# A decoder block on one core: the first modulation vectors divided between TensorE and VectorE, and GpSimd's share of that phase given to VectorE and ScalarE

## The chip, the cores and the metric

The kernel runs on one core of a Trainium2 chip. The metric is the device time of one execution in microseconds (us), lower is better. The times shown are device times of whole executions; the profile is of one further execution.

## The reference

One decoder block on x of 512 tokens by 2048 channels, all in float32. A conditioning vector c gives six modulation vectors, of which the first two (shift and scale) are needed before anything else can be projected. Cut to what the change touches:

```python
c_act = silu(c)
mod = c_act @ w_ada + b_ada                    # 2048 x 12288
sh1, sc1, gt1, sh2, sc2, gt2 = split(mod, 6)
h = rms_norm(x, g_mix) * (1 + sc1) + sh1
z = h @ w_in                                   # 2048 x 11344
# z is cut into q, k, v of two attention branches, an indexer's q and k, gates
...
```

Two attention branches, their gated merge, an output projection and a gated feed-forward with a depthwise convolution follow; the change leaves all of them alone.

## The kernel before

Activations stand transposed: a tile is 128 channels by 512 tokens, and there are 16 such channel tiles (the contraction tiles k of w_in). Every float32 product is made of three matmuls (`mm3`, lines 330 to 332): each factor is split into a rounded part h and a remainder l, and h·h, h·l and l·h are summed. ScalarE makes the rounded part of a weight tile (`convert`, L227), and another engine subtracts (L228): GpSimd where the unit is marked `early`, VectorE elsewhere.

The first phase, `first_*` and `hidden`, is a pipeline over the 16 channel tiles in nine groups (`GR`: one tile, seven times two, one). A group g needs the two modulation vectors of its own channels only, and then does a first part of the products for four column blocks of w_in (`FIRST`, in the order given by `ORD`): the indexer's first 512 columns, its 80 columns of k and w, its second 512 columns, and 512 columns of q and k of the first pair of heads. That is 13 output tiles of 128 (one of 80) columns by 512 tokens. Five of the 13 stay in PSUM over all groups ("stay"); eight are taken out of PSUM after each group and added to a copy in SBUF (`evac`, with `late` holding the one that is still to be taken out). PSUM has eight banks.

The modulation vectors of a group are c_act times 16 blocks of w_ada: one block per k, each 128 partitions by 2 vectors by 256 columns (for a group of two). `first_ada` is a generator that handles one block (or two half-size ones) per step. Before the change a step multiplies the block by its c value per partition on VectorE and adds it to one of two accumulators (L670, L672, scalar_tensor_tensor); at the end the two are added (L676). Only in group 0 the first `PK` = 10 blocks go to TensorE instead (L696). `hidden` then sums the accumulator over partitions on TensorE with a column of ones as the moving operand (L696, matmuls of one column; a float32 matmul has two records in the profile), adds the bias (L698), makes the scale (L700), and ScalarE applies scale and shift to the normalised tile `xr` twice (L705 for the rounded part, L711 in place); `hidden_rest_` subtracts (L721). `scaled` makes `xr` by multiplying with the norm (L652): the first two on VectorE, the others on GpSimd.

What sets the order: instructions stand on each engine's queue in the order in which the Python program issues them; nothing reorders them. `paced` runs steps of `first_ada` after each column block, so that the steps of group g+1 are spread over the column blocks of group g; `LEAD` says how many steps it is ahead. `hidden` of the next group is issued after two of the four column blocks of a group (`OF` = 2), `hidden_rest_` after three. Weight loads (`load`, L192) and w_ada loads (`first_load`, L288) are both on SyncE's queue; w_ada is loaded up to `AHEAD` = 10 blocks ahead, w_in three units ahead into three buffers. `evac` takes a tile from PSUM in two ways: for four of the eight keys VectorE adds straight from PSUM (L737), for the other four ScalarE copies (L740) and GpSimd adds (L741).

Of the kernel before, what the change touches and what calls it, by code (L numbers as in the profile page):

```python
# [14 lines left out]
OP = mybir.AluOpType  # L15
# [21 lines left out]
TAB = 640  # L37
NSLOT = 65
AHEAD = 20
LEAD = 8  # L40
AHEAD = 10
OF = 2
SP0 = 22
# [43 lines left out]
PK = 10  # L87
# [17 lines left out]
def block_kernel(ctx, tc, x, c, w_ada, b_ada, g_mix, w_in, w_o_sb, w_o_dsa, w_out, rel_bias,  # L105
                 g_ffn, w_gate, w_up, conv_w, conv_b, w_down, g_final, buckets, out, dbg=None):
    nc = tc.nc
    x, w_ada, w_in, w_o_sb, w_o_dsa, w_out = x[0], w_ada[0], w_in[0], w_o_sb[0], w_o_dsa[0], w_out[0]
# [15 lines left out]
    def T(dt=F32):  # L124
        return slots.tile([128, 512], dt, tag="slot", name="slot")

    def ps():
        return psum.tile([128, 512], F32, tag="ps", name="ps")
# [11 lines left out]
    def U(w, k0, nk, c0, nn, fn, early=False):  # L140
        steps.append(((w, k0, nk, c0, nn, early), fn))
        units.append(steps[-1][0])
# [9 lines left out]
    def F(fn):  # L152
        steps.append((None, fn))
# [5 lines left out]
    def advance(q, n=1):  # L159
        while q and n > 0:  # L160
            try:
                next(q[0])
                n -= 1
            except StopIteration:
                q.pop(0)
# [111 lines left out]
    GROUPS = [(sum(GR[:i]), sum(GR[:i + 1])) for i in range(len(GR))]  # L277
# [5 lines left out]
    def first_load(n):  # L283
        while len(first_raw) < min(n, len(first_cols)):
            k0, k1, k, nk = first_cols[len(first_raw)]
            raw = T().rearrange("p (k v n) -> p k v n", k=nk, v=2)
            for i in range(nk):
                nc.sync.dma_start(raw[:, i], wav2[:, k + i, SH1:SC1 + 1, 128 * k0:128 * k1])  # L288
            first_raw.append(raw)
# [6 lines left out]
    ones = const.tile([128, 128], F32, name="ones")  # L296
# [32 lines left out]
    def mm3(o, sh, sl, mh, ml, start, stop, skip=False):  # L329
        nc.tensor.matmul(o, lhsT=sh, rhs=mh, start=start, stop=False, skip_group_check=skip)  # L330
        nc.tensor.matmul(o, lhsT=sh, rhs=ml, start=False, stop=False, skip_group_check=skip)  # L331
        nc.tensor.matmul(o, lhsT=sl, rhs=mh, start=False, stop=stop, skip_group_check=skip)  # L332
# [221 lines left out]
    fin = []  # L554
# [64 lines left out]


    hT, xT, xr, xT_d = [], [], [], []
    rb1, direct = [], []
    modv2 = modv[:, 0:2 * KT].rearrange("p (v a) -> p v a", v=2)

    def first_norm():
# [22 lines left out]
    def scaled(d1):  # L648

        for d in range(len(xr), min(d1, KT)):  # L650
            xr.append(T())
            (nc.vector if d < 2 else nc.gpsimd).tensor_mul(xr[d], xT[d], rb1[0])  # L652

    fin, seen = [], [0]

    def first_ada():

        for n, (k0, k1, k, nk) in enumerate(first_cols):
            first_load(n + min(AHEAD, 22 - len(hT)))
            if k == 0:  # L660
                acc = []
            for i in range(nk):
                a = first_raw[n][:, i]
                c = c_act[:, k + i:k + i + 1]
                if k0 == 0 and k + i < PK:

                    direct.append((a, c))
                elif len(acc) < 2:
                    acc.append(T()[:, 0:256 * (k1 - k0)].rearrange("p (v n) -> p v n", v=2))
                    nc.vector.tensor_scalar(acc[-1], a, c, None, op0=OP.mult)  # L670
                else:
                    nc.vector.scalar_tensor_tensor(acc[i + k & 1], a, c, acc[i + k & 1], op0=OP.mult, op1=OP.add)  # L672
            first_raw[n] = None
            if k + nk == KT:
                if k0 > 1:
                    nc.vector.tensor_add(acc[0], acc[0], acc[1])  # L676
                    acc.pop()
                fin.append(acc)
            seen[0] += 1
            yield  # L680

    def hidden(k0, k1):

        while not fin:
            advance(back)
        acc = fin.pop(0)
        while late:
            evac(*late.pop())
        n = k1 - k0
        p = ps()  # L690
        terms = direct + [(a, ones[:, 0:1]) for a in acc]
        direct.clear()
        for m, (a, c) in enumerate(terms):
            for v in range(2):
                for i in range(n):
                    nc.tensor.matmul(p[:, v * n + i:v * n + i + 1], lhsT=a[:, v, 128 * i:128 * (i + 1)], rhs=c,  # L696
                                     start=m + v + i == 0, stop=m == len(terms) - 1, skip_group_check=True)
        nc.vector.tensor_add(modv2[:, :, k0:k1], p[:, 0:2 * n].rearrange("p (v a) -> p v a", v=2),  # L698
                             vecs[:, 0:2 * KT].rearrange("p (v a) -> p v a", v=2)[:, :, k0:k1])
        nc.vector.scalar_tensor_tensor(smix[:, k0:k1], modv[:, SC1 * KT + k0:SC1 * KT + k1], 1.0,  # L700
                                       vecs[:, 96 + k0:96 + k1], op0=OP.add, op1=OP.mult)
        for d in range(k0, k1):
            s, b = smix[:, d:d + 1], modv[:, SH1 * KT + d:SH1 * KT + d + 1]
            h, l, u = T(F32R), T(F32R), xr[d]
            nc.scalar.activation(h, u, AF.Identity, scale=s, bias=b)  # L705
            if d == 0:
                y = T()
                nc.vector.tensor_scalar(y, u, s, b, op0=OP.mult, op1=OP.add)
                u = y
            else:  # L710
                nc.scalar.activation(u, u, AF.Identity, scale=s, bias=b)  # L711
            rest.append((l, u, h))
            xr[d] = None
            hT.append((h, l))
# [3 lines left out]
    def hidden_rest_():  # L718
        while rest:
# [5 lines left out]
    FIRST = [(C_QIX, 512, [(2, 256, 128, False), (3, 384, 128, False), (0, 0, 128, True), (1, 128, 128, True)]),  # L725
             (C_QIX + 512, 512, [(6, 256, 128, False), (7, 384, 128, False), (4, 0, 128, True), (5, 128, 128, True)]),
             (C_KIX, 80, [("kw", 0, 80, True)]),
             ((C_QSB, C_KSB), 512, [("q0", 0, 128, False), ("q1", 128, 128, False), ("k0", 256, 128, False), ("k1", 384, 128, False)])]
    part, late = {}, []
    FIRST = [FIRST[i] for i in ORD]  # L730

    def evac(key, p, gi, w):
        if gi == 0:
            part[key] = T()
            nc.scalar.copy(part[key][0:w, :], p)
        elif key in (2, 6, "q0", "k0"):
            nc.vector.tensor_add(part[key], part[key], p)  # L737
        else:
            t = T()
            nc.scalar.copy(t, p)  # L740
            nc.gpsimd.tensor_add(part[key], part[key], t)  # L741

    def first_go(h, l, gi, tiles):
        k0, k1 = GROUPS[gi]
        for key, off, w, stay in tiles:
            if not stay:
                p = ps()[0:w, :]
            elif gi == 0:
                p = part[key] = ps()[0:w, :]
            else:  # L750
                p = part[key]
            for k in range(k0, k1):
                mm3(p, h[:, k - k0, off:off + w], l[:, k - k0, off:off + w], *hT[k],
                    k == 0 if stay else k == k0, k == KT - 1 if stay else k == k1 - 1)
            if late:
                evac(*late.pop())
            if not stay:
                late.append((key, p, gi, w))

    def spill(d1):  # L760

        for d in range(len(xT_d), min(d1, len(xr))):
            xT_d.append(dram.tile([128, 512], F32, name=f"xT{d}"))
            nc.sync.dma_start(xT_d[d], xT[d])
            xT[d] = None

    def paced(gi, i):

        goal = base[gi + 1] + LEAD
        if gi + 1 < len(GROUPS):  # L770
            goal += (i + 1) * (base[gi + 2] - base[gi + 1]) // (len(FIRST) - OF + 1)
        while seen[0] < min(goal, base[-1]):
            advance(back)

    base = [sum(16 // (2 // (b - a)) for a, b in GROUPS[:g]) for g in range(len(GROUPS) + 1)]
# [15 lines left out]
    for gi, (k0, k1) in enumerate(GROUPS):  # L791
        for i, (c0, nn, tiles) in enumerate(FIRST):
            if i == len(FIRST) - OF and gi + 1 < len(GROUPS):
                F(lambda g=gi + 1: hidden(*GROUPS[g]))
            if i == len(FIRST) - OF2:
                F(hidden_rest_)
            U(w_in, k0, k1 - k0, c0, nn, lambda h, l, gi=gi, tiles=tiles: first_go(h, l, gi, tiles), True)
            F(lambda gi=gi, i=i: paced(gi, i))
            F(lambda d=k1 + 4: scaled(d))
            F(lambda d=4 * gi + i - SP0: spill(d))  # L800

# [666 lines left out]
    acc = {}  # L1468
# [226 lines left out]
    held, last = [], []  # L1695
# [61 lines left out]
```

## Time and profile before

| | |
|---|---|
| time, median of 3 runs | 3073.22 us (3072.06 to 3073.41) |
| profiled execution, its own time | 3069.46 us |
| its span in the profile | 3067.7 us |
| mean granted TensorE clock | 0.967 of 2.4 GHz |
| busy: PE, VectorE (DVE), ScalarE (ACT), GpSimd (POOL) | 94%, 85%, 40%, 17% |
| first phase (to the last of its tile products) | to 269.3 us |
| data moved by DMA | 477.7 MB |

PE is TensorE's matmuls, PEld its weight loads, PEclk the clock that was granted to TensorE as a share of full speed (it has two levels, 1.2 and 2.4 GHz; 0.50 is the lower). In a timeline a row has start and length of a run of equal instructions in us, and in square brackets how long its engine stood idle before it and for whom. A matmul's length overlaps the next one's start, so its pace is read from start to start.

### The profile page before, as it was taken

How to read it: one execution, taken by the hardware profiler on the slowest of the kernel's cores; microseconds unless marked ns; L12 is line 12 of the kernel's file. 1: busy time of each engine (PE TensorE's matmuls, PEld its weight loads, DVE VectorE, ACT ScalarE, POOL GpSimd, SP SyncE). 2: the span in 40 equal slices, each digit the busy share in tenths (PEclk: the TensorE clock that was granted, in tenths of full speed). 3: DMA queues.
4: the chain of work that ended last, by engine and by line, in shares of the span. 5: the costliest groups of instructions: out<-in, count | busy, mean ns of one | idle time of the engine just before them, and what ended most of it. 6: DMA issues, size and time to landing. Idle time of an engine off the chain costs nothing. (4 is left out here: it accounts for less than half of the span.)

```text
span 3067.7 us, 51328 instructions
## 1 busy us (share of the span) xinstructions
PE 2886.7 (94%) x20195; PEld 2709.7 (88%) x20195; DVE 2604.4 (85%) x3538; ACT 1222.2 (40%) x1482; POOL 514.1 (17%) x406
## 2 busy tenths in 40 slices
PE   7779999999999999999988999999999989989887
PEld 5557888888888999888988999999999989989886
DVE  7985797888888887459989999989999999898998
ACT  4224433323235434224445444444444443343434
POOL 4653122201112000000123000000000022131524
PEclk7889999999999999999989999999999999999998
DMA  9654327787763445543452333333333344444555
GB/s 298 194 172 123 91 89 238 236 269 258 232 225 106 132 132 166 185 145 110 147 176 93 122 118 117 118 118 118 118 119 123 121 127 131 138 137 160 180 174 176
DMA packets 382274, 477.74 MB, mean 156 GB/s; under 512 B 27855, under 2 KB 269903, under 8 KB 382031
## 3 DMA queue, kind: packets, MB, share of 16 engines
q1 hardware_dynamic: 375119, 461.87, 47.0%
q10 hardware_dynamic: 6912, 12.59, 1.1%
q8 instruction: 158, 2.59, 0.4%
q14 instruction: 85, 0.70, 0.1%
HBM read 425.05 MB, written 51.92 MB: 155 GB/s over the span
## 5 line engine op out<-in xcount | busy, mean ns | idle before, releaser
L331 PE MATMUL ps<-slot,wh 128*128 128x256 f32 (+2 forms) x4624 | 1435.4, 310 | 21.4 <-DVE slot L413 16.7
L330 PE MATMUL ps<-slot,wh 128*128 128x256 f32 (+2 forms) x4624 | 1438.3, 311 | 13.5 <-DVE slot L737 8.7
L332 PE MATMUL ps<-slot,wl 128*128 128x256 f32 (+2 forms) x4624 | 1433.4, 310 | 13.6 <-DVE wl L224 13.6
L331 PEld LDWEIGHTS ps<-slot,wh 128*128 128x128 f32 (+1 forms) x4624 | 893.3, 193 | 68.5 <-DVE slot L413 18.4
L330 PEld LDWEIGHTS ps<-slot,wh 128*128 128x128 f32 (+1 forms) x4624 | 893.7, 193 | 59.9 <-DVE slot L737 11.1
L332 PEld LDWEIGHTS ps<-slot,wl 128*128 128x128 f32 (+1 forms) x4624 | 892.9, 193 | 60.0 <-DVE wl L224 15.6
L223 ACT CAST wh<-raw 128x1792 fp32r<-128x1792 f32 x338 | 570.7, 1693 | 732.8 <-PE ps L331 233.8
L224 DVE TENSOR_TENSOR wl<-raw,wh 128x1792 fp32r<-128x1792 f32 x338 | 688.6, 2038 | 68.9 <-ACT wh L223 68.6
L330 PE MATMUL ps<-wh,slot 128*128 128x256 f32 (+1 forms) x1708 | 502.2, 294 | 32.3 <-DVE slot L448 22.4
L331 PE MATMUL ps<-wl,slot 128*128 128x256 f32 (+1 forms) x1708 | 498.9, 292 | 22.8 <-DVE wl L224 22.4
L332 PE MATMUL ps<-wh,slot 128*128 128x256 f32 (+1 forms) x1708 | 497.2, 291 | 4.7 <-DVE slot L497 4.7
L330 PEld LDWEIGHTS ps<-wh,slot 128*128 128x128 f32 x1708 | 335.4, 196 | 41.9 <-DVE slot L448 23.8
L331 PEld LDWEIGHTS ps<-wl,slot 128*128 128x128 f32 x1708 | 335.9, 197 | 28.6 <-DVE wl L224 25.5
L332 PEld LDWEIGHTS ps<-wh,slot 128*128 128x128 f32 x1708 | 335.8, 197 | 9.4 <-DVE slot L497 7.5
L227 ACT CAST wh<-raw 128x1024 fp32r<-128x1024 f32 (+3 forms) x178 | 177.6, 998 | 248.6 <-PE ps L331 172.0
L228 DVE TENSOR_TENSOR wl<-raw,wh 128x1024 fp32r<-128x1024 f32 x142 | 181.0, 1276 | 52.0 <-ACT wh L227 51.9
L205 DVE TENSOR_TENSOR raw<-raw 128x512 f32<-128x512 f32 x256 | 178.7, 698 | 26.3 <-DMA raw<-in_w_up_dram 9.0
L1588 POOL TENSOR_TENSOR slot<-slot 128x256 f32<-128x256 f32 x22 | 28.5, 1295 | 1018.9 <-PE ps L332 849.2
L528 DVE SCALAR_TENSOR_TENSOR slot<-slot,c_act 128x512 f32<-128x512 f32 x240 | 191.6, 798 | 6.8
L672 DVE SCALAR_TENSOR_TENSOR slot<-slot,c_act 128x512 f32<-128x512 f32 (+1 forms) x116 | 139.1, 1261 | 0.7 <-DMA slot<-in_w_ada_dram 0.7
L207 DVE TENSOR_TENSOR raw<-raw 128x256 f32<-128x256 f32 x256 | 121.3, 474 | 8.8
L206 DVE TENSOR_TENSOR raw<-raw 128x256 f32<-128x256 f32 x256 | 117.6, 459 | 8.8
(224 smaller groups left out, 2518.5 us busy)
## 6 DMA issues: line engine op xcount, KB each, us to landing
slot<-in_w_ada_dram SPq DMA_DIRECT2D x368, 256.0 KB, 4.8
raw<-in_w_in_dram SPq DMA_DIRECT2D x118, 512.0 KB, 4.8
raw<-in_w_gate_dram SPq DMA_DIRECT2D x176, 256.0 KB, 3.1
raw<-in_w_up_dram SPq DMA_DIRECT2D x176, 256.0 KB, 3.1
raw<-in_w_down_dram SPq DMA_DIRECT2D x88, 512.0 KB, 4.1
raw<-in_w_in_dram SPq DMA_DIRECT2D x114, 256.0 KB, 2.9
raw<-in_w_out_dram SPq DMA_DIRECT2D x64, 256.0 KB, 3.2
slot<-g SPq DMA_DIRECT2D x56, 256.0 KB, 4.7
```

The costliest lines, as they stand in the source:

```text
L205: nc.vector.tensor_add(b[:, :, 2:4], b[:, :, 5:7], shared)
L206: nc.vector.tensor_add(b[:, :, 1], b[:, :, 3], b[:, :, 5])
L207: nc.vector.tensor_add(b[:, :, 0], b[:, :, 4], b[:, :, 1])
L223: nc.scalar.copy(hf, f)
L224: nc.vector.tensor_sub(l.rearrange("p (q f) -> p q f", q=n), f, hf.bitcast(F32))
L227: nc.scalar.copy(h, r)
L228: (nc.gpsimd if kind else nc.vector).tensor_sub(l, r, h.bitcast(F32))
L330: nc.tensor.matmul(o, lhsT=sh, rhs=mh, start=start, stop=False, skip_group_check=skip)
L331: nc.tensor.matmul(o, lhsT=sh, rhs=ml, start=False, stop=False, skip_group_check=skip)
L332: nc.tensor.matmul(o, lhsT=sl, rhs=mh, start=False, stop=stop, skip_group_check=skip)
L528: nc.vector.scalar_tensor_tensor(acc, raw[n], s, acc, op0=OP.mult, op1=OP.add)
L672: nc.vector.scalar_tensor_tensor(acc[i + k & 1], a, c, acc[i + k & 1], op0=OP.mult, op1=OP.add)
```

## The change

In the first modulation vectors, of every 8 blocks those with k modulo 8 equal to 1, 4 or 6 go to TensorE for all groups but the first: four matmuls of one column (two in the last group), with the block as stationary operand and c's column as moving operand, summed in one PSUM bank that stays open while the group's steps run. VectorE keeps the other five in one accumulator, without the last addition. `hidden` adds the accumulator's own column sums into the same bank. `paced` is now called after every output tile, not after every column block, and its steps are divided over 13 tiles; while the next group's `hidden` has not been issued, it stops at that group's last step. `LEAD` is 10.

The units of the phase lose the mark `early`, so the remainders of w_in (L228) are subtracted on VectorE. `scaled` runs on VectorE alone. `evac` copies with ScalarE for all eight keys and adds on VectorE. No work of the phase is left on GpSimd.

```diff
-LEAD = 8
+LEAD = 10
...
-            (nc.vector if d < 2 else nc.gpsimd).tensor_mul(xr[d], xT[d], rb1[0])
+            nc.vector.tensor_mul(xr[d], xT[d], rb1[0])
...
+    ON_PE = (1, 4, 6)
+
+    def on_pe(p, a, c, first=False, last=False):
+        w = a.shape[2] // 128
+        for j in range(2 * w):
+            nc.tensor.matmul(p[:, j:j + 1], lhsT=a[:, j // w, 128 * (j % w):128 * (j % w + 1)], rhs=c,
+                             start=first and j == 0, stop=last, skip_group_check=True)
...
             if k == 0:
-                acc = []
+                acc, p, first = None, ps(), True
...
-                if k0 == 0 and k + i < PK:
-
-                    direct.append((a, c))
-                elif len(acc) < 2:
-                    acc.append(T()[:, 0:256 * (k1 - k0)].rearrange("p (v n) -> p v n", v=2))
-                    nc.vector.tensor_scalar(acc[-1], a, c, None, op0=OP.mult)
+                if k + i < PK if k0 == 0 else (k + i) % 8 in ON_PE:
+                    on_pe(p, a, c, first)
+                    first = False
+                elif acc is None:
+                    acc = T()[:, 0:256 * w].rearrange("p (v n) -> p v n", v=2)
+                    nc.vector.tensor_scalar(acc, a, c, None, op0=OP.mult)
                 else:
-                    nc.vector.scalar_tensor_tensor(acc[i + k & 1], a, c, acc[i + k & 1], op0=OP.mult, op1=OP.add)
+                    nc.vector.scalar_tensor_tensor(acc, a, c, acc, op0=OP.mult, op1=OP.add)
...
-                if k0 > 1:
-                    nc.vector.tensor_add(acc[0], acc[0], acc[1])
-                    acc.pop()
-                fin.append(acc)
+                fin.append((p, acc, first))
+                p = acc = None
...
-        p = ps()
-        terms = direct + [(a, ones[:, 0:1]) for a in acc]
-        direct.clear()
-        for m, (a, c) in enumerate(terms):
...
+        on_pe(p, acc, ones[:, 0:1], first, True)
...
     def evac(key, p, gi, w):
+        t = T()
+        nc.scalar.copy(t[0:w, :], p)
         if gi == 0:
-            part[key] = T()
-            nc.scalar.copy(part[key][0:w, :], p)
-        elif key in (2, 6, "q0", "k0"):
-            nc.vector.tensor_add(part[key], part[key], p)
+            part[key] = t
         else:
-            t = T()
-            nc.scalar.copy(t, p)
-            nc.gpsimd.tensor_add(part[key], part[key], t)
+            nc.vector.tensor_add(part[key], part[key], t)
...
             if not stay:
                 late.append((key, p, gi, w))
+            paced(gi)
...
-    def paced(gi, i):
-
-        goal = base[gi + 1] + LEAD
-        if gi + 1 < len(GROUPS):
-            goal += (i + 1) * (base[gi + 2] - base[gi + 1]) // (len(FIRST) - OF + 1)
+    def paced(gi):
+
+        if gi + 1 == len(GROUPS):
+            return
+        steps_of[gi] = steps_of.get(gi, 0) + 1
+        goal = base[gi + 1] + LEAD + steps_of[gi] * (base[gi + 2] - base[gi + 1]) // sum(len(f[2]) for f in FIRST)
+        if len(hT) < GROUPS[gi + 1][1]:
+            goal = min(goal, base[gi + 2])
         while seen[0] < min(goal, base[-1]):
             advance(back)
...
-            U(w_in, k0, k1 - k0, c0, nn, lambda h, l, gi=gi, tiles=tiles: first_go(h, l, gi, tiles), True)
-            F(lambda gi=gi, i=i: paced(gi, i))
+            U(w_in, k0, k1 - k0, c0, nn, lambda h, l, gi=gi, tiles=tiles: first_go(h, l, gi, tiles))
```

## Rows read from the trace of the kernel before

**Rows 1.** The span in 40 equal slices of 76.7 us: busy share in tenths of PE and VectorE, and the granted clock.

```profile
PE   7779999999999999999988999999999989989887
DVE  7985797888888887459989999989999999898998
...
PEclk7889999999999999999989999999999999999998
```

**Rows 2.** Busy time of each engine by stretch: the stretch, its length, busy us and number of instructions of PE, PEld, DVE, ACT and POOL, then granted clock, DMA share and GB/s. The stretches up to 269.32 run from one bias addition of `hidden` (L698) to the next, the one before 269.32 to the end of the phase; the last is what follows the phase.

```profile
30.28:47.45 17.17, 10.29 (x32) 8.02 (x33) 14.72 (x23) 2.60 (x4) 10.01 (x4) 0.60 1.09 350
47.45:70.69 23.24, 17.09 (x63) 13.58 (x64) 22.01 (x23) 10.12 (x15) 14.78 (x7) 0.79 0.95 301
70.69:100.72 30.03, 21.56 (x87) 17.08 (x88) 26.26 (x25) 8.66 (x12) 18.55 (x10) 0.84 0.67 213
...
192.16:221.28 29.12, 22.25 (x87) 17.57 (x88) 25.87 (x28) 8.76 (x12) 16.50 (x9) 0.85 0.69 202
221.28:248.72 27.44, 22.63 (x83) 17.81 (x84) 15.90 (x21) 8.65 (x12) 12.47 (x8) 0.83 0.25 82
248.72:269.32 20.60, 20.16 (x88) 15.79 (x87) 10.17 (x12) 9.47 (x15) 14.36 (x11) 1.00 0.58 161
...
269.32:1000.00 730.68, 724.17 (x4310) 643.43 (x4311) 601.59 (x986) 285.57 (x490) 131.92 (x141) 0.99 0.58 190
```

**Rows 3.** Who waited for whom in the first 300 us: us in total, times, longest.

```profile
PE ps L696 <- DVE slot L676: 42.3, 6, 7.7
```

**Rows 4.** Groups of instructions between 60 and 262 us by line, engine and shape: count, busy us, mean ns of one, idle before.

```profile
L672 DVE SCALAR_TENSOR_TENSOR slot<-slot,c_act 128x512 f32<-128x512 f32 x75 | 109.3, 1517 | 0.0
...
L228 POOL TENSOR_TENSOR wl<-raw,wh 128x1024 fp32r<-128x1024 f32 x19 | 49.1, 2585 | 61.6 <-ACT wh L227 51.9 <-issue 9.7
L741 POOL TENSOR_TENSOR slot<-slot 128x512 f32<-128x512 f32 x28 | 44.6, 1599 | 18.3 <-ACT slot L740 17.4 <-DMA raw<-in_w_in_dram 0.8
...
L227 ACT CAST wh<-raw 128x1024 fp32r<-128x1024 f32 x19 | 19.8, 1044 | 22.4 <-PE ps L331 18.6 <-POOL slot L741 1.9 <-DMA slot<-in_w_ada_dram 1.9
L737 DVE TENSOR_TENSOR slot<-slot,ps 128x512 f32<-128x512 f32 x29 | 19.2, 679 | 23.2 <-PE ps L332 20.8 <-ACT slot L705 2.5
...
L740 ACT COPY slot<-ps 128x512 f32<-128x512 f32 x28 | 16.4, 586 | 45.2 <-PE ps L332 38.3 <-DVE slot L672 3.5 <-DMA slot<-in_w_ada_dram 3.1
...
L676 DVE TENSOR_TENSOR slot<-slot 128x512 f32<-128x512 f32 x6 | 6.2, 1028 | 0.2
```

**Rows 5.** Timeline of VectorE between 22 and 75 us: start, length, line and number of equal instructions in a run.

```profile
22.16 1.29 DVE L652 TENSOR_TENSOR slot<-slot 128x512 f32<-128x512 f32 x2
...
34.24 0.87 DVE L670 TENSOR_SCALAR slot<-slot,c_act 128x512 f32<-128x512 f32 x2
35.03 9.35 DVE L672 SCALAR_TENSOR_TENSOR slot<-slot,c_act 128x512 f32<-128x512 f32 x14
...
52.90 9.00 DVE L672 SCALAR_TENSOR_TENSOR slot<-slot,c_act 128x512 f32<-128x512 f32 x5
```

**Rows 6.** Timeline of VectorE behind the phase, where it makes the same remainders for later units.

```profile
279.99 1.23 DVE L228 TENSOR_TENSOR wl<-raw,wh 128x1024 fp32r<-128x1024 f32 x1 [1.59 <-ACT wh L227]
```

**Rows 7.** Timeline of TensorE at the full clock: two of a tile's matmuls, and a run of eight records of one-column matmuls with the tile matmul behind it.

```profile
60.63 0.39 PE L331 MATMUL ps<-slot,wh 128*128 128x512 f32 x1
60.86 0.39 PE L332 MATMUL ps<-slot,wl 128*128 128x512 f32 x1
...
511.62 1.00 PE L561 MATMUL ps<-ones,slot 128*128 128x1 f32 x8
512.49 0.48 PE L330 MATMUL ps<-slot,wh 128*128 128x512 f32 x1
```

**Rows 8.** The same at the lower clock, around `hidden` of one group.

```profile
98.85 1.84 PE L696 MATMUL ps<-ones,slot 128*128 128x1 f32 x8 [7.08 <-DVE slot L676]
100.55 0.77 PE L330 MATMUL ps<-slot,wh 128*128 128x512 f32 x1
...
101.12 0.63 PE L331 MATMUL ps<-slot,wh 128*128 128x512 f32 x1
101.55 0.63 PE L332 MATMUL ps<-slot,wl 128*128 128x512 f32 x1
```

**Rows 9.** Busy time by short stretches, with the columns of rows 2.

```profile
20.00:22.00 2.00, 1.73 (x16) 1.76 (x16) 1.28 (x5) 0.73 (x2) 0.00 (x0) 1.00 1.17 286
22.00:24.00 2.00, 2.00 (x14) 2.00 (x13) 1.97 (x6) 0.00 (x0) 0.00 (x0) 0.64 1.00 267
...
92.00:98.00 6.00, 0.00 (x0) 0.00 (x0) 5.97 (x6) 0.00 (x0) 4.10 (x2) 0.69 0.21 50
...
114.00:116.00 2.00, 1.45 (x6) 1.24 (x7) 2.00 (x3) 0.94 (x2) 1.47 (x1) 1.00 1.04 360
```

**Rows 10.** Timeline of the start, several engines: the first casts of w_in, their remainders, three of the tiles `xr`, the first use of the vectors and the first remainder product.

```profile
26.42 1.46 ACT L227 CAST wh<-raw 128x512 fp32r<-128x512 f32 x3 [5.69 <-DMA raw<-in_w_in_dram]
...
27.12 2.80 POOL L228 TENSOR_TENSOR wl<-raw,wh 128x512 fp32r<-128x512 f32 x3 [24.68 <-ACT wh L227]
29.88 3.89 POOL L652 TENSOR_TENSOR slot<-slot 128x512 f32<-128x512 f32 x3
...
31.25 0.81 ACT L705 ACTIVATE slot<-slot,modv,smix 128x512 fp32r<-128x512 f32 x1 [3.38 <-DVE smix L700]
...
34.37 0.80 PE L331 MATMUL ps<-slot,wh 128*128 128x512 f32 x1 [1.46 <-DVE slot L721]
```

More of the change, by code (lines that the diff above doesn't have):

```diff
@@ L621, in block_kernel @@
     hT, xT, xr, xT_d = [], [], [], []
-    rb1, direct = [], []
+    rb1 = []
     modv2 = modv[:, 0:2 * KT].rearrange("p (v a) -> p v a", v=2)
@@ L659, in first_ada @@
             first_load(n + min(AHEAD, 22 - len(hT)))
+            w = k1 - k0
             if k == 0:
-                acc = []
+                acc, p, first = None, ps(), True
             for i in range(nk):
@@ L685, in hidden @@
             advance(back)
-        acc = fin.pop(0)
+        p, acc, first = fin.pop(0)
         while late:
@@ L689, in hidden @@
         n = k1 - k0
-        p = ps()
-        terms = direct + [(a, ones[:, 0:1]) for a in acc]
-        direct.clear()
-        for m, (a, c) in enumerate(terms):
[L694 to L697, printed above, removed]
+        on_pe(p, acc, ones[:, 0:1], first, True)
         nc.vector.tensor_add(modv2[:, :, k0:k1], p[:, 0:2 * n].rearrange("p (v a) -> p v a", v=2),
@@ L765, in spill @@
             xT[d] = None
-    def paced(gi, i):
-        goal = base[gi + 1] + LEAD
-        if gi + 1 < len(GROUPS):
-            goal += (i + 1) * (base[gi + 2] - base[gi + 1]) // (len(FIRST) - OF + 1)
+    steps_of = {}
+    def paced(gi):
[5 more added lines that the diff above has]
+            goal = min(goal, base[gi + 2])
         while seen[0] < min(goal, base[-1]):
```

## The prediction

> **What bounds the kernel now.** I read the page's slices first [rows 1]: the first four hold a TensorE that is 70 to 90% busy at a granted clock of 0.7 to 0.9, and a VectorE at 70 to 90%. Behind the phase TensorE is busy for 724.2 of 730.7 us at 0.99 [rows 2]. So what the phase saves, the end of the kernel saves, and nothing else in the diff touches the later 2800 us.
>
> Then the stretches from one group's vectors to the next [rows 2]. From 70.69 to 221.28 us they are five equal periods, 150.6 us, 30.1 each. In one, VectorE is busy 26 us, TensorE 21.6 us at a mean clock of 0.84, DMA share is 0.6 to 0.7. VectorE ends the period: TensorE stood 42.3 us in six waits for its last addition [rows 3], and VectorE's own idle is mostly the answer of the matmuls behind it. In these waits TensorE's clock falls (0.69 on average over a 6 us gap with no matmul at all [rows 9]) and the next products start at the lower one.
>
> Why is VectorE so slow? The same multiply-add took 9.35/14 = 0.67 us while GpSimd was idle and 9.00/5 = 1.80 us while GpSimd worked [rows 5]; 1.52 us is the mean of the phase [rows 4]. The fast run lies in a stretch where DMA moved 350 GB/s [rows 2], so it isn't DMA that slows it. GpSimd is busy 18.6 us of a period.
>
> **The change, part by part, for one period of a two-tile group.**
>
> VectorE loses 6 of 16 block steps and the last addition (1.03 us, rows 4), four additions from PSUM (4 x 0.68, rows 4), and the slowdown. It keeps 1 multiply (0.87/2 = 0.44) and 9 multiply-adds at 0.67: 6.5 us. It gains 8 additions from SBUF, for which I take the product of two SBUF tiles of that size, 1.29/2 = 0.645 [rows 5]: 5.2; two products of `scaled`, 1.3; and three remainders of 128x1024 at 1.23 [rows 6] with a small one that I put at 0.3 (the 160 columns scaled from that row, rounded up): 4.0. The two L721 cost 1.3, bias and scale 0.3. Sum 18.6 us, against 26.
>
> TensorE: 13 tiles x 2 channel tiles x 3 = 78 products at a pace of 0.227 (60.63 to 60.86, rows 7): 17.7 us. One-column matmuls: 6 blocks x 4, and 4 in `hidden`, 28, each two records; eight records took 511.62 to 512.49 = 0.87 us [rows 7], so 7 x 0.87 = 6.1 us. Sum 23.8 us at the full clock. At the lower clock a product takes 0.43 and eight records 1.70 [rows 8]: 33.3 + 7 x 1.7 = 45.2.
>
> ScalarE: three casts at 1.04 [rows 4] and a small one, about 0.3, 4 activations at 0.81 [rows 10], 8 copies at 0.59 [rows 4]: about 11.4 us. DMA: 16 blocks of 262 KB and 2 x 128 x 1616 columns x 4 B = 5.85 MB; at the 350 GB/s of rows 2, 16.7 us. So TensorE becomes the bound, by its own work, at 23.8.
>
> On that come waits. `hidden` still waits for VectorE's last step, k = 15, which stands behind a remainder that waits for a cast, which waits for the end of the unit before: 1.04 + 1.23 + 0.67 plus about 0.3 of semaphores, 3.2 us after that end, while TensorE has one small tile (1.36) and one block (0.87) to do: about 1.0 us of waiting. PSUM has five resident tiles and the open bank of the vectors, so two banks are left to rotate. A tile's copy may start when the tile ends; at a group's first unit it stands behind a cast on ScalarE (1.04 + 0.59, against a tile of 1.36): 0.3 to 0.6 us. No other wait is on the path, since evacuation no longer goes through VectorE's queue. Period: 25.5 us. From below 24.2 (only half of these waits), from above 28 (a wait of that kind in each of the four units).
>
> Five periods: 150.6 - 5 x 25.5 = 23.1 saved. The next stretch (27.44, rows 2) has 78 products and 6 blocks of half size: 17.7 + 2.6 + 0.4 = 20.8, with the waits 22.0: 5.4 saved. The tail of 20.60 us is dense already at clock 1.00: nothing.
>
> **The start loses.** `ahead()` puts three remainders on VectorE's queue in front of `scaled` and of the first group's steps. Their casts wait for w_in until 26.42 [rows 10], so VectorE, which now did its first steps from 22 on, stands until 27.1. Then come 1.5 us of remainders, 4 x 0.645 of `scaled`, and six half-size steps at about 0.43 (an estimate: half of 0.67 and a tenth), 2.6: 33.8 us. `hidden` of group 0 follows at once; its vectors are there at about 35.2, not 30.28. From there the chain is shorter, because nothing contends: the first remainder product starts at about 37.4, not 34.37 [rows 10]. Then, with `LEAD` 10, eleven steps of group 1 are issued behind the first tile, four of them matmul blocks, and two more before `hidden` of group 1. At the lower clock, 4 tiles at 1.28 and 6 x 1.7 behind tile one: vectors of group 1 at about 55, not 47.45; if the clock rises midway, 50. I take a loss of 6 us (bounds 1 and 8). The next stretch (23.24 now, 6 of them a wait for VectorE) fills its wait with 6 blocks: even.
>
> Sum: 23.1 + 5.4 - 6 = 22.5 us off the profiled execution's 3069.46 (span 3067.7 and 1.8 around it): 3047. That execution was 3.8 us below the median of the three timed runs; from the median, 3050.7. I forecast 3050.
>
> **A row and a rule on TensorE's clock.** In this trace one-column matmuls do let the clock fall: a long run of them, beginning at 21.2 us after little work, had it at 1.00 before 22 us and at 0.64 in the next two [rows 9], while the engine counted as fully busy. Against that, a stretch that was only 1.45 of 2.00 us busy with tile products held 1.00 [rows 9], and eight records between dense products did no harm [rows 7]. The change's steps are 0.87 us each between tiles of 1.36. The Trainium skill (TensorE: Matmul & The Clock Gate, A second HAM failure mode: psum-queue depth-cycling) says that short idle spells between groups of matmuls can be enough to make the clock swing between its levels, and that the price then shows in throughput. The trace neither shows nor excludes this for steps of this length; it is the rival on the other side below.
>
> **Rivals.**
> - *The clock falls between the steps (slower).* Place: the steady periods, 26% of whose work is one-column matmuls. Price: a period wholly at the lower clock costs 45.2 instead of 23.8. With a share f of it low, a period is 25.5 + 21.4 f; the gain is gone at 29.3, so from f = 0.18 on. At f = 0.3 a period is 32: about 3090. For it: the fall at 22 us, and the low clock that the phase starts with. Against it: the clock held at 73% busy. Chance 0.11.
> - *VectorE and ScalarE in turn hold TensorE at every unit.* Period 28: 150.6 - 140 + 3 - 6 = 7.6 saved, 3065. For it: in-order queues with more on VectorE, which then waits for copies and casts. Against: 18.6 us of 25. Chance 0.16.
> - *The waits nearly vanish and the clock is up early.* Period 24.2, last stretch 21, start -1: 29.6 + 6.4 - 1 = 35 saved, 3038. Chance 0.17.
> - DMA as the bound needs under 16.7 us a period, which TensorE's 23.8 doesn't allow; I give it no chance of its own.
>
> **How the numbers follow.** The forecast has 0.56; its own range is 3040 to 3060 (start 1 to 8, period 24.7 to 27). About 0.2%, 6 us, is what a measurement of this kernel can tell from no change. Faster by more than that: 0.56 + 0.17 + two thirds of 0.16 = 0.84. Within: 0.06, the rest of the second rival and a little of the first. Slower: 0.10. The range 3033 to 3070 leaves out the clock rival (0.11) and some 0.06 below.
>
> **What would show it.** In the changed profile: multiply-adds at 0.67 and GpSimd idle in the phase; periods of 25.5 between bias additions, VectorE busy under 20 of them, TensorE nearly all; clock near 1.00; group 0's bias addition at 35 and group 1's at 50 to 55; the phase's end near 247 instead of 269. Wrong if the clock in the periods is under 0.9, if the one-column steps take more than 0.9 us each, if TensorE waits over 2 us per period, or if the time after the phase changes.

## The result, and the profile after

The changed kernel took 3050.54 us in the median of four runs (3044.51 to 3055.13), the kernel before 3072.64; the ratio is 0.9928 with a 95% interval of 0.9907 to 0.995. The forecast was 3050 in a range of 3033 to 3070. The profiled execution of the changed kernel is the slowest of its four (3055.13 us, span 3053.2), so the two profiles differ by 14.5 us where the medians differ by 22. One profiled execution among the experiments (8221 us, of e10_two_12) was disturbed and isn't read.

The slices of the changed kernel's page, which answer to [rows 1]:

```profile
PE   7999999999999999999988999999999989989897
DVE  5666888888878887469989989988998998898998
...
PEclk7999999999999999999989999999999999999998
```

TensorE is now busy for 9 tenths in the second to the fourth slice, and VectorE fell from 7 to 9 tenths to 5 or 6 in the first three. So the bound of the phase has changed hands, as forecast.

The stretches from one bias addition of `hidden` to the next, with the columns of [rows 2] and in the same order; the last line is the first part of the tail:

```profile
36.45:56.61 20.16, 18.84 (x72) 16.81 (x73) 9.92 (x16) 2.60 (x4) 0.00 (x0) 0.50 0.80 250
56.61:81.54 24.93, 24.26 (x111) 20.66 (x112) 14.74 (x23) 10.79 (x16) 0.00 (x0) 0.77 0.67 210
81.54:108.21 26.67, 26.00 (x135) 21.89 (x135) 18.18 (x28) 10.89 (x16) 0.00 (x0) 0.94 0.70 221
108.21:134.88 26.67, 26.00 (x135) 21.88 (x135) 18.18 (x29) 10.89 (x16) 0.00 (x0) 0.94 0.70 221
134.88:159.96 25.08, 24.41 (x135) 20.72 (x135) 18.00 (x28) 10.91 (x16) 0.00 (x0) 1.00 0.73 233
159.96:186.62 26.66, 25.99 (x135) 21.86 (x135) 18.20 (x28) 10.89 (x16) 0.00 (x0) 0.94 0.71 221
186.62:214.09 27.47, 26.13 (x135) 21.95 (x135) 17.49 (x27) 10.90 (x16) 0.00 (x0) 0.94 0.66 208
214.09:237.34 23.25, 23.21 (x108) 18.94 (x108) 14.53 (x26) 10.90 (x16) 0.00 (x0) 0.93 0.42 127
237.34:258.00 20.66, 20.66 (x98) 17.11 (x97) 13.61 (x23) 13.75 (x23) 0.00 (x0) 1.00 0.66 198
```

Read the third column against the length: TensorE is busy 26.0 of 26.67 us. Read the clock: 0.94 in four of the five periods, 1.00 in one, and that one is 1.6 us shorter than three of the others with the same 135 matmul records (the fifth, 27.47 us, has a second wait of 0.68 us). The account, profile against profile: group 1's vectors 9.2 us later (56.61 for 47.45), the next stretch 1.7 longer, five periods 18.0 shorter (132.55 for 150.59), the next 4.2 shorter, the tail to the first product of the next phase 1.1 shorter (it starts at 256.79, for 269.32). That is 12.5 us; the other 2.0 lie behind the phase.

What happens at the end of each group's steps stands in the timelines of TensorE and of VectorE, here of one period. First TensorE, from the last tile before `hidden` to the first behind it:

```profile
105.28 0.39 PE L332 MATMUL ps<-slot,wl 128*80 128x512 f32 x1
105.51 0.95 PE L661 MATMUL ps<-c_act,slot 128*128 128x1 f32 x8
107.12 1.05 PE L661 MATMUL ps<-ones,slot 128*128 128x1 f32 x8 [0.67 <-DVE slot L681]
108.04 0.48 PE L330 MATMUL ps<-slot,wh 128*128 128x512 f32 x1
```

Then VectorE:

```profile
105.18 1.23 DVE L228 TENSOR_TENSOR wl<-raw,wh 128x1024 fp32r<-128x1024 f32 x1 [1.10 <-ACT wh L227]
106.32 0.75 DVE L681 SCALAR_TENSOR_TENSOR slot<-slot,c_act 128x512 f32<-128x512 f32 x1
108.21 0.16 DVE L698 TENSOR_TENSOR modv<-ps,vecs 128x4 f32<-128x4 f32 x1 [1.15 <-PE ps L661]
```

VectorE stood 1.10 us for a cast of w_in, made the remainder, and only then the last block step; TensorE waited 0.67 us for it. For 2.5 us, from the block at 105.51 to the tile at 108.04, TensorE had no tile product. Behind it the clock falls, here in short stretches of the same view:

```profile
108.00:109.00 1.00, 1.00 (x6) 0.87 (x6) 0.32 (x2) 0.39 (x1) 0.00 (x0) 1.00 0.95 334
109.00:110.00 1.00, 1.00 (x4) 0.72 (x4) 0.00 (x0) 0.97 (x2) 0.00 (x0) 0.50 1.07 379
110.00:111.00 1.00, 1.00 (x4) 0.81 (x3) 0.00 (x0) 0.97 (x2) 0.00 (x0) 0.50 1.04 347
111.00:112.00 1.00, 1.00 (x3) 0.79 (x3) 0.00 (x0) 1.00 (x2) 0.00 (x0) 0.50 1.07 366
112.00:113.00 1.00, 1.00 (x8) 0.87 (x6) 0.21 (x1) 1.00 (x2) 0.00 (x0) 0.80 0.95 312
```

The fall costs the 1.6 us by which the periods differ. A wait of the same 0.67 us stands in front of each of the five periods; four of them begin with such a fall and one, from 134.88 on, does not.

And the start. VectorE's timeline, against [rows 10]:

```profile
22.54 0.69 DVE L594 COPY slot<-ps 128x512 f32<-128x512 f32 x1 [0.72 <-PE ps L590]
28.58 1.49 DVE L228 TENSOR_TENSOR wl<-raw,wh 128x512 fp32r<-128x512 f32 x3 [5.35 <-ACT wh L227]
29.99 2.49 DVE L652 TENSOR_TENSOR slot<-slot 128x512 f32<-128x512 f32 x4
...
36.45 0.16 DVE L698 TENSOR_TENSOR modv<-ps,vecs 128x2 f32<-128x2 f32 x1 [1.11 <-PE ps L661]
```

VectorE stands for 5.35 us in front of the remainders, for a cast that itself waits for w_in:

```profile
27.93 1.42 ACT L227 CAST wh<-raw 128x512 fp32r<-128x512 f32 x3 [6.10 <-DMA raw<-in_w_in_dram]
```

What stands behind the remainders on VectorE's queue is late by it: the first vectors come 6.2 us later than before. This is the second place that the change made. Some 1.5 us of the delay are the casts' own, which began at 26.42 before [rows 10].

### The profile page after: what moved, and what is told of

The parts are those of the page before. It is cut to its first block, busy times and chain, and to the rows that moved or that the text cites. A ratio compares the mean times of both kernels' runs of the same rounds, so it can differ in the third digit from the quotient of the medians.

```text
span 3053.2 us, 51934 instructions
## 1 busy us (share of the span) xinstructions
PE 2919.4 (96%) x20543; PEld 2748.3 (90%) x20543; DVE 2553.0 (84%) x3565; ACT 1238.7 (41%) x1514; POOL 368.4 (12%) x324
## 5 line engine op out<-in xcount | busy, mean ns | idle before, releaser
L228 DVE TENSOR_TENSOR wl<-raw,wh 128x1024 fp32r<-128x1024 f32 (+3 forms) x178 | 211.0, 1187 | 111.0 <-ACT wh L227 110.9
L1246 POOL TENSOR_TENSOR mask<-mask,slot 128x512 f32<-128x512 f32 x13 | 19.0, 1460 | 552.5 <-ACT slot L1245 552.0
```

The source lines that it names most:

```text
L228: (nc.gpsimd if kind else nc.vector).tensor_sub(l, r, h.bitcast(F32))
```

## The experiments

Theory A: GpSimd had made VectorE slow; freed of that and of a part of the blocks, VectorE is quick enough, and TensorE with its clock is the bound. Rival B: only the blocks that moved to TensorE gained. Others are named where they first appear. Each kernel was timed beside the kernel before, and its ratio to it is given with its 95% interval; the expectations are quoted as written before the runs.

### The two halves of the change: e1_no_pe and e2_gpsimd_back

```diff
-    ON_PE = (1, 4, 6)
+    ON_PE = ()
```

> The changed kernel with no block on TensorE (all 16 multiply-adds of a group on VectorE, in one accumulator), GpSimd still idle in the phase. Theory A (VectorE was slowed by GpSimd; without GpSimd it is quick enough, and TensorE's own 23.8 us and its clock are the new bound): VectorE's period is its 18.2 us after the change and 6 more multiply-adds of 0.74, 22.6; TensorE 17.7 + 0.9 and a wait of some 4 us before each column sum with a fall of the clock, 25 to 26 us a period; the start gains some 3 us as no blocks stand between the first tiles. About the time after the change, 3043 to 3055. Theory B (the gain is the blocks that moved to TensorE): back to the kernel before, 3065 or more.

Measured: 3060.58 us, ratio 0.9969 (0.9958 to 0.998). The periods are 28.5 us, with VectorE busy 22.07 of them, as worked out (22.6), and TensorE waiting 40.4 us in six waits for VectorE's last step, its clock at 0.80 to 0.87. So without the blocks on TensorE a period gains 1.7 us on the 30.1 of before, not 4 to 5. The time lies between the ranges of both theories. VectorE was quick enough by its sum, but not by its place in the order. This kernel and the next keep the change's pacing (`paced` after every tile, `LEAD` 10) and its single accumulator; what these are worth by themselves was not tried.

```diff
-            nc.vector.tensor_mul(xr[d], xT[d], rb1[0])
+            (nc.vector if d < 2 else nc.gpsimd).tensor_mul(xr[d], xT[d], rb1[0])
...
+        if gi > 0 and key in (2, 6, "q0", "k0"):
+            nc.vector.tensor_add(part[key], part[key], p)
+            return
         t = T()
         nc.scalar.copy(t[0:w, :], p)
...
-            nc.vector.tensor_add(part[key], part[key], t)
+            nc.gpsimd.tensor_add(part[key], part[key], t)
...
-            U(w_in, k0, k1 - k0, c0, nn, lambda h, l, gi=gi, tiles=tiles: first_go(h, l, gi, tiles))
+            U(w_in, k0, k1 - k0, c0, nn, lambda h, l, gi=gi, tiles=tiles: first_go(h, l, gi, tiles), True)
```

> The changed kernel with GpSimd's work of the phase put back (remainders, 14 of the 16 scaled tiles, four of eight additions, the other four straight from PSUM on VectorE), blocks on TensorE as changed. Theory A: multiply-adds go back from 0.70 to about 1.5 us, but only 10 of 16 are left, so VectorE is busy about 9 x 1.5 + 5.5 = 19 us of a period and GpSimd 18.6; TensorE's 23.8 stays the bound, waits grow by 1 to 3 us a period: 3055 to 3068. Theory B: as after the change, 3045 to 3055.

Measured: 3035.14 us, ratio 0.9887 (0.9872 to 0.9903). Neither expected it: this half alone is faster than the whole change, by 0.0041 of 3071 us, some 12.6 us. (The two profiles are 22.9 us apart: each shows one execution, here of 3032.03 us and there of 3055.13.) The stretches of its profile, to be held against those of the changed kernel:

```profile
0.00:28.90 28.90, 18.67 (x117) 17.12 (x117) 15.95 (x41) 16.99 (x43) 2.16 (x11) 0.95 0.86 259
28.90:47.16 18.26, 15.81 (x72) 14.06 (x73) 12.59 (x15) 2.85 (x5) 8.55 (x7) 0.61 1.07 346
47.16:66.56 19.40, 18.83 (x111) 16.22 (x111) 12.60 (x16) 10.14 (x15) 12.00 (x7) 1.00 0.97 312
66.56:90.85 24.29, 24.29 (x135) 20.65 (x135) 13.47 (x18) 8.66 (x12) 16.00 (x11) 1.00 0.82 258
90.85:115.14 24.29, 24.29 (x135) 20.65 (x135) 14.50 (x18) 8.66 (x12) 17.17 (x11) 1.00 0.76 242
```

TensorE is busy in every microsecond of these periods, the clock is 1.00, the first vectors come at 28.9 us and not at 36.45. The contention is back and does no harm:

```profile
L681 DVE SCALAR_TENSOR_TENSOR slot<-slot,c_act 128x512 f32<-128x512 f32 x44 | 45.7, 1038 | 0.7
...
L734 DVE TENSOR_TENSOR slot<-slot,ps 128x512 f32<-128x512 f32 x20 | 13.7, 685 | 28.4 <-PE ps L332 28.4
```

A multiply-add takes 1.04 us (0.745 in the changed kernel), but there are ten blocks instead of 16, and VectorE has 10 us to spare in a period. The additions from PSUM, which have one operand in SBUF, still take 0.685. The Trainium skill (SBUF — State Buffer, Who interferes with whom) has it so: two operands in SBUF contend with GpSimd's reads, one does not. The trace agrees: a multiply-add takes 1.04 beside GpSimd's work against 0.745 without it, and an addition from PSUM 0.685 beside it (0.679 before [rows 4]), no longer than the change's addition from SBUF takes without GpSimd, 0.686.

So rival B is right on the sign of the halves: the blocks on TensorE gain, and taking GpSimd out on top of it costs. By ratios: 9.5 us gained by GpSimd's half alone, 35 by TensorE's, 22 by both, each with the new pacing.

### What stands at the end of a group's steps: e3_lead12 and e4_two_of_eight

```diff
-LEAD = 10
+LEAD = 12
```

> The changed kernel with LEAD 12 instead of 10: the last steps of the next group are issued one tile earlier, so block k = 14 stands one tile away from the column sums, and VectorE has finished k = 15 when TensorE comes to them. Theory A: the clock falls after the column sums because block, wait and sums make about 2.5 us with no tile product in a row; now only the sums (0.87 us) are left in a row, no fall, no wait, periods of 24.2 instead of 26.7: 3036 to 3043 and little spread between runs. Rival C (the clock falls because a quarter of the whole period is one-column matmuls, wherever they stand): the falls stay, periods 26 to 26.7, 3046 to 3053.

Measured: 3035.68 us, ratio 0.9893 (0.9877 to 0.9909), 10.7 us better than the change by ratios.

```profile
71.91:96.12 24.21, 24.21 (x135) 20.66 (x135) 18.04 (x30) 10.89 (x16) 0.00 (x0) 1.00 0.75 243
96.12:120.32 24.20, 24.20 (x135) 20.65 (x135) 18.08 (x28) 10.90 (x16) 0.00 (x0) 1.00 0.75 243
120.32:144.53 24.21, 24.21 (x135) 20.65 (x135) 18.09 (x28) 10.90 (x16) 0.00 (x0) 1.00 0.76 243
```

The same work on the same engines, only issued one tile earlier, and four periods are 24.2 as expected, without wait or fall (the fifth is 25.0, with a wait of 0.51 us and no fall). The same 135 records, 56 of them of one-column matmuls, keep the clock at 1.00, so rival C, which lays the fall to their share, falls. The periods are not all of the gain in the profile: they make 10.7 us of it, and 9.6 were there before them, as group 2's vectors come at 71.91 us, for 81.54. The stretch in front of them is at a clock of 1.00 here (52.90:71.91, shown with e9 below) and was at 0.77 in the change. Whether the earlier steps brought the clock up sooner isn't shown. The spread between runs didn't shrink (3031.95 to 3041.76), against the expectation; where it comes from isn't shown either, as only one execution is profiled.

```diff
-    ON_PE = (1, 4, 6)
+    ON_PE = (1, 5)
```

> The changed kernel with two blocks of eight (k modulo 8 equal to 1 or 5) on TensorE instead of three. Theory A (TensorE is the bound of a period): 2 blocks of 0.87 us less on TensorE, 2 multiply-adds of 0.74 more on VectorE; the last block is k = 13, a tile away from the sums, so the clock holds more often: a period 1.7 to 3 us shorter, 3032 to 3043. Rival D (the chain of VectorE and ScalarE with its waits sets the period): VectorE gets 1.5 us more, the period grows by about 1: 3055 to 3060.

Measured: 3040.52 us, ratio 0.9901 (0.9887 to 0.9915). Its five periods lie between 24.6 and 26.3 us, three of them at a clock of 1.00 and about 24.7. Two of them:

```profile
124.90:149.65 24.75, 22.59 (x119) 18.79 (x119) 19.24 (x30) 10.90 (x16) 0.00 (x0) 1.00 0.74 238
149.65:175.25 25.60, 24.22 (x119) 19.93 (x119) 19.59 (x31) 10.89 (x16) 0.00 (x0) 0.93 0.73 229
```

Better than the change, as theory A had it, but TensorE is busy only 22.6 of 24.75 us in these: it waits 11.1 us in six waits for VectorE's last step. Less work on TensorE is taken back in part by the same place in VectorE's order; rival D has a share in it. In the two other periods the clock fell (0.91 and 0.93), here without a block right before the wait. So the block beside the sums isn't needed for a fall. A wait stands in front of each of the two, of 2.5 and 2.2 us; but waits of 1.4 to 2.2 us stand in front of the other three as well, which kept 1.00.

### The start, and GpSimd in parts: e6_start_back, e7_remainders_back, e5_gpsimd_two, e8_rem_two_12

```diff
-            nc.vector.tensor_mul(xr[d], xT[d], rb1[0])
+            (nc.gpsimd if d in (2, 3) else nc.vector).tensor_mul(xr[d], xT[d], rb1[0])
...
-            U(w_in, k0, k1 - k0, c0, nn, lambda h, l, gi=gi, tiles=tiles: first_go(h, l, gi, tiles))
+            U(w_in, k0, k1 - k0, c0, nn, lambda h, l, gi=gi, tiles=tiles: first_go(h, l, gi, tiles), gi == 0)
```

> The changed kernel, with GpSimd's work put back at the start alone: the remainders of group 0's units and two of the scaled tiles. Theory F (what GpSimd's removal costs has two places: the start, where VectorE now waits for w_in and its casts, and the periods, where a remainder stands in front of the last block step): the start's 7.5 us come back (first vectors at 29 to 30, not 36.5), the periods stay 25 to 26.7 with their falls of the clock: 3040 to 3046. Rival G (the start doesn't matter, since DMA or TensorE holds the next groups anyway): within 3 us of the change, 3048 to 3053.

Measured: 3045.17 us, ratio 0.9919 (0.9905 to 0.9933). The first vectors come at 27.79 us, 8.7 earlier than in the change; at group 2 5.2 us of it are left (76.29 for 81.54), and the periods are 25.1 or 26.7 as before. By medians 5 us better than the change, by ratios 3; the intervals of the two overlap. The trace goes theory F's way, but the times alone don't show a gain. The wait of 0.67 us stands in front of each of its five periods too, and only two of them begin with a fall.

```diff
-            U(w_in, k0, k1 - k0, c0, nn, lambda h, l, gi=gi, tiles=tiles: first_go(h, l, gi, tiles))
+            U(w_in, k0, k1 - k0, c0, nn, lambda h, l, gi=gi, tiles=tiles: first_go(h, l, gi, tiles), True)
```

> The changed kernel with only the remainders of w_in (L228) back on GpSimd; scaled tiles and additions stay on VectorE, copies on ScalarE, LEAD 10. Theory F: both places are the remainders', so this is as quick as all of GpSimd's work put back: first vectors at about 30, no wait before the column sums, 24.3 us a period at the full clock, 3032 to 3039. Rival H (the additions and scaled tiles on VectorE cost as much): 3042 to 3050.

Measured: 3048.33 us, ratio 0.9925 (0.9913 to 0.9938). Theory F's number was wrong by 9 us at least, and the time lies in rival H's range. The start came back (30.0 us), but the periods are not 24.3 (24.3, 26.5, 25.8, 27.3 and 26.6). The groups of instructions between 70 and 190 us show what became slower:

```profile
L738 DVE TENSOR_TENSOR slot<-slot 128x512 f32<-128x512 f32 x37 | 42.8, 1173 | 25.4 <-ACT slot L734 25.3
L228 POOL TENSOR_TENSOR wl<-raw,wh 128x1024 fp32r<-128x1024 f32 x14 | 35.6, 2540 | 79.6 <-ACT wh L227 72.5 <-DMA slot<-in_w_ada_dram 7.1
L681 DVE SCALAR_TENSOR_TENSOR slot<-slot,c_act 128x512 f32<-128x512 f32 x41 | 34.8, 848 | 0.2
```

The additions, which the change moved to SBUF operands, take 1.17 us beside GpSimd's remainders in the mean (0.686 in the change), eight of them a period. Before the change four of them read PSUM on VectorE and four were GpSimd's. Half of each division is no better than the change's and, by ratios, some 12 us worse than GpSimd's whole share (e2_gpsimd_back). That the additions are what makes it so wasn't tried by itself.

Both edits that follow, on top of e2_gpsimd_back:

```diff
-LEAD = 10
+LEAD = 12
...
-    ON_PE = (1, 4, 6)
+    ON_PE = (1, 5)
```

> GpSimd's work put back as in e2_gpsimd_back, two blocks of eight on TensorE instead of three, LEAD 12. In e2_gpsimd_back TensorE was busy all of 24.29 us a period at the full clock, VectorE only 14.5. Theory A: TensorE is the bound there, so two blocks of 0.87 us less make 22.6 us a period, VectorE 14.5 + 2 x 1.04: six periods, 10 us less than e2: 3024 to 3030. Rival D (VectorE and its waits set the period as soon as it gets more): 24.3 or more, 3034 to 3040.

> Remainders back on GpSimd, two blocks of eight on TensorE, LEAD 12; scaled tiles and additions on VectorE as changed. Theory A with F: TensorE 22.6 us a period and the bound, VectorE 18.1 - 4.0 + 1.5 = 15.6 and some contention with GpSimd's 7 us: 3022 to 3030. Rival D: VectorE's waits set 24 us or more, 3032 to 3040.

(e8 is e7_remainders_back with the same two lines.) Measured: e5 3046.84 us, ratio 0.9926 (0.9912 to 0.9939); e8 3046.70 us, 0.9922 (0.9909 to 0.9936). Both lie above the ranges of theory A and of rival D. In e8 the periods are 26.0 to 30.3 us. In e5 they are 24.4 to 30.2 us: VectorE has two more of the slowed multiply-adds (1.12 us) in its queue, and TensorE waits for additions from PSUM to set a bank free:

```profile
PEld ps L330 <- DVE slot L734: 15.8, 6, 3.7
PE ps L330 <- DVE slot L734: 13.2, 6, 3.2
```

In the three periods with such a wait of 2.4 to 3.2 us the clock is 0.83 to 0.88; in the two with one of 1.4 to 1.5 us it held 1.00. Two blocks fewer on TensorE would have saved 1.7 us a period; one wait of 2.4 to 3.2 us and the fall behind it took 4 to 6.

### Put together: e9_lead12_start, e11_group1, e10_two_12 and e12_two_12_again

On top of e6_start_back:

```diff
-LEAD = 10
+LEAD = 12
```

> The changed kernel with LEAD 12 and, as in e6_start_back, GpSimd's work put back at the start alone. Theory F (two places, independent of each other: the start and the end of each group's steps): both gains add, e3's 15 us and e6's 5 us: 3027 to 3033, periods of 24.2 at the full clock, first vectors at 28. Rival G: the start's gain is lost behind LEAD 12 (more steps behind the first tile), 3034 to 3039.

Measured: 3037.03 us, ratio 0.9899 (0.9884 to 0.9915): no better than e3_lead12. The first vectors come at 28.99 us (35.02 in e3), group 1's at 50.84 (52.90), group 2's at 72.73 (71.91). The stretches of e9, where the gain went:

```profile
28.99:50.84 21.85, 19.23 (x72) 16.96 (x73) 11.86 (x16) 2.60 (x4) 6.44 (x6) 0.50 0.98 314
50.84:72.73 21.89, 21.89 (x111) 18.48 (x112) 14.83 (x22) 10.89 (x16) 0.00 (x0) 0.86 0.83 267
```

The same stretches of e3:

```profile
35.02:52.90 17.88, 16.56 (x72) 14.97 (x73) 10.01 (x16) 2.60 (x4) 0.00 (x0) 0.58 0.79 252
52.90:71.91 19.01, 19.01 (x111) 16.07 (x111) 14.54 (x22) 10.80 (x16) 0.00 (x0) 1.00 0.96 309
```

The records are equal in number, 72 and 111, and the clock is not: 0.50 and 0.86 against 0.58 and 1.00. The earlier start was spent at the lower clock.

On top of e9_lead12_start:

```diff
-                if k + i < PK if k0 == 0 else (k + i) % 8 in ON_PE:
+                if k + i < PK if k0 == 0 else k0 > 1 and (k + i) % 8 in ON_PE:
```

> e9_lead12_start with group 1's blocks all on VectorE (TensorE takes its three of eight from group 2 on). In the start the six blocks of group 1 run at the lower clock, 1.7 us each, with four output tiles behind them, while VectorE stands. Theory: without them group 1's vectors come at 43 to 45 us, not 49, held by DMA and VectorE; 3 to 5 us less than e9: 3023 to 3029. Rival (the clock starts the next stretch lower because TensorE did less before, and gives the gain back): no change to e9, within 2 us.

Measured: 3037.77 us, ratio 0.9903 (0.9887 to 0.9918), no difference to e9. Group 1's vectors come at 49.39 us, not at 43 to 45, because now TensorE waits 9.2 us for VectorE; and the next stretch runs at 0.66 and takes 27.67 us. Here the rival was right.

On top of the changed kernel itself:

```diff
-LEAD = 10
+LEAD = 12
...
-    ON_PE = (1, 4, 6)
+    ON_PE = (1, 5)
```

> The changed kernel with LEAD 12 and two blocks of eight on TensorE, nothing on GpSimd. In e4_two_of_eight (LEAD 10) TensorE waited 1.8 us a period for VectorE's last step. Theory A: with the steps a tile earlier that wait is gone and TensorE's 22.6 us is the period: 7 us less than e3_lead12, 3026 to 3031. Rival D (VectorE, 19.3 us busy and in order, sets the period with two blocks): 24 us or more, 3034 to 3042.

> The kernel of e10_two_12 once more, whose profiled execution was disturbed (8219 us). Its four other times lie between 3029.7 and 3036.1. Theory A: periods of 22.6 to 23 us, TensorE busy throughout, and 3026 to 3033. Rival D: periods of 24 us with TensorE waiting for VectorE's last step, 3030 to 3037, no difference to e3_lead12 that can be measured.

Measured: e10 ratio 0.9884 (0.9864 to 0.9903); e12 3033.03 us (3032.51 to 3033.23), 0.9884 (0.9863 to 0.9906). The periods of e12:

```profile
95.85:119.49 23.64, 22.98 (x120) 18.69 (x119) 19.24 (x31) 10.80 (x16) 0.00 (x0) 1.00 0.78 249
119.49:143.14 23.65, 22.92 (x120) 18.73 (x119) 19.25 (x31) 10.81 (x16) 0.00 (x0) 1.00 0.78 248
```

They are 23.65 us, between theory A's 22.6 to 23 and rival D's 24: TensorE is busy 1.2 us less than in e3 and stands 0.7 us waiting for VectorE's last step, so 0.56 us a period is left of the two blocks' 1.7. It is the lowest median of all kernels, 17.5 us under the change by medians and 13.5 by ratios, but its interval overlaps those of e2 and e3.

## Why the prediction was right, and where it wasn't

**That TensorE becomes the bound: right.** VectorE's 18.6 us measured 18.2, ScalarE's 11.4 measured 10.9, TensorE's 23.8 measured 24.2 where nothing waits (e3_lead12). A remainder took 1.23, a multiply-add by itself 0.745 (the 0.67 taken was the pace within a run), a step of eight records 0.81 for 0.87 (101.05 to 101.85 us in e3_lead12).

**The wait before the column sums: right in place, mis-sized in price.** The step "about 1.0 us of waiting" measured 0.67, but I let it cost only its own length. Behind it the clock fell in four of five periods, which is another 1.6. Its "about 0.3 of semaphores" had no row; measured, the hand-overs are 0.04 us from the cast to the remainder and 0.05 from the last step to the sums (the cast ends at 105.14 us; the rest stands in the rows of the period above). The wait of 0.3 to 0.6 for a PSUM bank came in one period of five, 0.68 us long. The period of 25.5 measured 25.1 without the fall and 26.7 with it, 26.5 in the mean. That 25.5 lies between is luck: the waits were over-estimated and the fall was left out. The terms as written add up to 25.1 to 25.4, not 25.5, and half of the waits would make some 24.5, not 24.2.

**The rival of the clock: half right.** Its place was wrong. It was laid to "the steady periods, 26% of whose work is one-column matmuls"; e3_lead12 has the same share and holds 1.00 in every period. In the periods of all kernels profiled, each fall begins in a wait of TensorE or behind one, and where the wait before the sums went (e2_gpsimd_back, e3_lead12) no fall was left. A wait isn't enough for one: of equal waits of 0.67 us some were followed by a fall and others not (the change, e6_start_back), e12_two_12_again has waits of 0.7 us and no fall, and e4_two_of_eight had one of 2.2 us with a fall behind it and one without. What decides between them isn't shown.

**"The start loses": right in direction, and more than its upper bound.** First vectors at 36.45 for 35.2, as the first casts began 1.5 us later than in [rows 10]; group 1's at 56.61 for "about 55", a loss of 9.2 us where I took 6 and gave bounds of 1 and 8. All of it ran at 0.50, as the upper bound had supposed. "Even" for the next stretch was 1.7 us short, at a clock of 0.77.

**Why VectorE was slow: the cause was right, a row was misread, and the conclusion was wrong.** GpSimd does slow the multiply-adds: 1.52 us beside it before, 0.75 without it. But in the quick run of [rows 5], from 35.03 to 44.38 us, GpSimd was not idle throughout:

```profile
39.78 6.52 POOL L228 TENSOR_TENSOR wl<-raw,wh 128x512 fp32r<-128x512 f32 x1 [6.01 <-DMA slot<-in_w_ada_dram]
```

VectorE's steps went on at 0.66 us beside it, and the one subtraction took 6.52 us, where three of that size took 2.80 in [rows 10]. It ended at 46.30 us, 1.1 us after VectorE's last step before a pause. So there it was GpSimd that was slowed; what decides which of the two it is isn't shown here. From the slow steps the prediction took that freeing VectorE of GpSimd is part of the gain. e2_gpsimd_back shows that it isn't: with ten blocks of 16 on VectorE, slowed steps no longer end the period. Taking GpSimd out then put two things on VectorE's queue that wait for casts, in front of the first vectors and in front of each group's last step, and as a whole cost some 12 us. That these two places are all of the 12 is argued: moving the second alone (e3_lead12) was worth 11, freeing the first alone (e6_start_back) no more than the times can tell, and both together (e9_lead12_start) no more than the second. The prediction had both places, the 5 us of the start and the remainder before k = 15, and counted them as dues of the change, without asking which half of the change they belong to.

**The sum.** Forecast 22.5 us off; the medians moved by 22.1. That they agree so closely is in part luck. In the profiles it is 14.5: the five periods gave 18.0 for 23.1, the next stretch 4.2 for 5.4, the start and the stretch behind it lost 10.9 for 6, and 3.1 came from the tail and behind the phase, which were put at nothing; the phase ended at 256.8 us and not at 247. The four executions took 3044.5 and 3047.1 us at a mean granted clock of 0.975 and 0.974, and 3054.0 and 3055.1, the profiled one, at 0.970 and 0.971. So the clock varies between executions; in which stretch, one profile can't tell. What decides the clock in the first 70 us, and so the spread between runs of one kernel, isn't settled by these runs.

## What to carry to other kernels

An engine that works in order isn't free because its sum of busy time is below the bound; look at what stands directly in front of the instruction for which the bound engine waits, and try to issue that chain a tile earlier before moving work between engines. LEAD 12 for 10 was worth 11 us here, nearly as much as giving GpSimd its work back (12.6). When a change has two halves, measure each alone: the halves here gained 9.5 and 35 us, and together 22. What both halves share, here the pacing, wants a run of its own, and none was made here.

## What the runs showed of the hardware

A wait of 0.67 us among one-column matmuls was followed, in four of five periods of the changed kernel and in two of five of e6_start_back, by 3 to 4 us at the lower clock (the short stretches above, 0.50 from 109 to 112 us), a price of 1.6 us for a period: more than twice the wait. An addition of two SBUF tiles took 0.686 us with GpSimd idle and 1.173 in the mean beside its subtractions (e7_remainders_back), while the same addition from PSUM took 0.685 beside them (e2_gpsimd_back). And the cost can fall on the other side: beside a run of VectorE's multiply-adds at their full pace one subtraction of 128x512 took GpSimd 6.52 us (kernel before, from 39.78 us).
